# Relative-bias rows between the first weight tiles, and both parts of x in one 512-column up projection, in a hybrid decoder layer

## The chip, the core and the metric

The kernel runs on one core of one Trainium2 chip. The metric is the device time of one execution in microseconds (us). The core has five engines with instruction streams of their own: TensorE (PE in the profile; matmuls, which write to PSUM), VectorE (DVE), ScalarE (ACT), GpSimd (POOL) and SyncE (SP, which here only issues DMAs). PEld is TensorE's loading of the stationary operand. An engine works through its stream in order and waits on semaphores that other engines and DMAs raise.

## What is computed

One layer of a hybrid decoder on 256 tokens of 1024 channels, all in fp32. In the notation of the reference, cut to what matters:

```python
def reference(x, rel_bias, ...):               # x: (1, 256, 1024), rel_bias: (32, 16)
    x = x + token_mixer(rms_norm(x, norm_mix_g), ..., rel_bias)
    x = x + squared_relu_mlp(rms_norm(x, norm_mlp_g), w_up, w_down)
    return rms_norm(x, final_norm_g)

def token_mixer(xn, ...):
    proj = xn @ w_in
    (qa, ka, va, qb, kb, vb, qi, ki, wi, xc, yc, gates) = split(proj)
    y_a = moba_attention(qa, ka, va, rel_bias[:, :8])       # 8 heads of 64
    y_b = dsa_attention(qb, kb, vb, qi, ki, wi, rel_bias[:, 8:])   # index logits qi.ki choose 64 keys
    y_c = rg_lru(causal_depthwise_conv(xc), ...) * gelu(yc)
    g = sigmoid(gates)
    merged = g[0] * (y_a @ w_pa) + g[1] * (y_b @ w_pb) + g[2] * (y_c @ w_pc)
    return merged @ w_o

def squared_relu_mlp(xn, w_up, w_down):        # 1024 -> 4096 -> 1024
    return square(relu(xn @ w_up)) @ w_down
```

To the logits of both attentions the bias `rel_bias[t5_bucket(t - s)]` is added: a row of the small table, chosen by the distance of query and key.

## The kernel before

**Products in three passes.** TensorE's fast fp32 form rounds its operands. So every operand is split in two: hi is the rounded value (a ScalarE copy, line 134), lo is what is left over (a VectorE subtraction, line 135). Each product is hi x hi, hi x lo and lo x hi (`PASSES`, line 189), all added up in one PSUM tile.

**Weights** come as 512 KB half tiles `raw` over SP's queue (`load`, line 142), five of which fit; ScalarE and VectorE split them to hi and lo, six each. One weight tile (two halves) serves one PSUM tile.

**Two layouts.** `fmajor` (line 191) keeps the weights stationary and streams the 256 tokens: output channels on the partitions, 256 columns a matmul, two halves `c` of 128 output channels next to one another in a PSUM tile of 512 columns; `ks` restricts it to some of the eight blocks k of 128 input channels. `tmajor` (line 203) streams 512 weight columns with the activations stationary; down projection (line 777) and gates do the like.

**Order.** A scheduler sets every engine's order by priorities and its own estimate of times; weights are raised by `AHEAD`, evacuations of PSUM by `EVAC`. Two stretches are in manual order: the start (line 288; all engines but SP), which builds the normalised input xnh and xnl, the index queries `ps_qi` of weight tiles 0 and 1, the index keys `ps_kw` and the norm's factors (y_n on GpSimd, line 323), and TensorE's part from the output projection into the MLP (line 721).

**Relative bias** (lines 359 to 379), outside the manual stretch: `tab` (32 x 16 values and a row of NEG) and `oh` (a one-hot matrix of buckets, 33 x 384) are loaded over SP's queue; ScalarE makes `ohr` and `tabh`, VectorE `tabl`; two matmuls `psr` of 384 columns give a row of biases for every head, 8 times over; VectorE copies it (`rrow`), and a DMA on GpSimd's queue writes it many times to a scratch table `toep` in HBM, from which `load_bias` reads shifted rows for the attentions.

**Index logits** `l_i` (lines 415 to 418) take the index queries and the keys `keysh`, `keysl`, made from `ki` by `pair_keys` on ScalarE and VectorE. The **recurrent branch** has conv tiles ps_xc, second-branch tiles ps_yc, and gate matmuls `ps_ri` (line 509) that take xch and xcl.

**Into the MLP.** `residual(t, h)` (line 692) adds the output projection to x, transposes four blocks on TensorE (`tp`, line 173), and forms x2h on ScalarE (line 180) and x2l on VectorE (line 186). The first two up projections are cut in two at k: blocks 0 to 3 of tile 0, then `residual(1, 1)`, blocks 0 to 3 of tile 1, then blocks 4 to 7 of both (lines 744 to 751).

**The MLP** runs over 16 groups g of 256 hidden channels. The up projection of a group is one tile `ps_up` (48 matmuls of 256 columns, line 199). `squares` (line 759): ScalarE Relu from PSUM, ScalarE Square to hh, VectorE product, VectorE difference hl. The down projection of group g - 2 follows: 24 matmuls of 512 columns into four tiles pd. Three PSUM accumulation tiles (`acc_tile`) take turns.

## Time and profile before

| | |
|---|---|
| runs of the kernel | 455.03, 454.80, 454.54 us; median 454.8 us |
| the profiled execution | 456.36 us, of which the span of the trace is 454.6 us |
| granted TensorE clock, mean | 0.999 |
| busy: TensorE, VectorE, ScalarE, GpSimd | 445.2 (98%), 338.0 (74%), 267.0 (59%), 24.6 (5%) us |
| chain of work that ended last | TensorE 92%, DMA 2%, VectorE 2%, ScalarE 2% |
| HBM | 81.11 MB read, 1.83 MB written, 182 GB/s over the span |

Busy times are sums over an engine's instructions in the profiled execution. The chain of work that ended last is followed back from the last instruction, at each step to what released it; here it runs along TensorE nearly throughout. In a timeline a row gives the start, the length of a run of like instructions with the modelled end of the last, the engine and line, out<-in, the number of instructions (x), and in brackets how long the engine was idle before and on whom it waited. Since matmuls are pipelined, the pace of one is read from starts, not from ends.

### The profile page before, as it was taken

The numbers are of one execution on the slowest core, as the hardware profiler recorded it, in microseconds if no ns is written. First come the engines' busy times: TensorE is split into PE (matmuls) and PEld (weight loads), VectorE is DVE, ScalarE is ACT, GpSimd is POOL, SyncE is SP. The second block draws the span as 40 slices with busy tenths as digits, with TensorE's granted clock in tenths as the row PEclk, the third lists the DMA queues.
The fourth block names the chain that finished last, engine by engine and source line by source line (L and its number), as shares of the span: only waits on it lengthen the run. The fifth ranks groups of instructions, "written<-read, shape, count | busy, mean of one in ns | idle before, by whom it ended". The sixth has DMA issues, their size and how long they took to land.

```text
span 454.6 us, 7382 instructions
## 1 busy us (share of the span) xinstructions
PE 445.2 (98%) x2738; PEld 400.6 (88%) x2738; DVE 338.0 (74%) x656; ACT 267.0 (59%) x442; POOL 24.6 (5%) x61
## 2 busy tenths in 40 slices
PE   8998999999999999999999999999999999999994
PEld 8997889989988888888888889999999999999984
DVE  6798989999989999965888586655555555555545
ACT  6848398865368789665644466444444444444453
POOL 5700030000010100000000000000000000000000
PEclk9999999999999999999999999999999999999999
DMA  7877857525855453545555744555555565555202
GB/s 261 326 242 272 264 174 236 180 96 175 272 163 181 138 187 117 201 154 177 186 175 189 231 160 149 185 189 190 189 184 191 188 189 187 192 187 190 81 1 92
DMA packets 23840, 83.42 MB, mean 184 GB/s; under 512 B 2987, under 2 KB 3020, under 8 KB 23804
## 3 DMA queue, kind: packets, MB, share of 16 engines
q1 hardware_dynamic: 22700, 80.05, 53.5%
q0 software_dynamic: 960, 2.88, 2.2%
q8 instruction: 21, 0.34, 0.3%
q14 instruction: 15, 0.12, 0.1%
q10 hardware_dynamic: 144, 0.02, 0.0%
HBM read 81.11 MB, written 1.83 MB: 182 GB/s over the span
## 4 chain that ended last, share of the span: by engine, by line
PE 92%; DMA 2%; DVE 2%; ACT 2%; issue 1%; ACTq 0%; DVEq 0%
PE ps_up L199 20%; PE pd L777 19%; PE ps_g L209 14%; PE ps_p L209 7%; PE po L209 5%; PE ps_qa L199 3%; PE ps_qb L199 3%; PE ps_ka L199 3%; PE ps_kb L199 3%; PE ps_vb L209 2%; PE ps_va L209 2%; PE ps_qi L304 2%; DMA raw<-wts 2%; PE ps_yc L199 2%; PE ps_qi L199 1%; DMA sp<-small 1%
## 5 line engine op out<-in xcount | busy, mean ns | idle before, releaser
L135 DVE TENSOR_TENSOR lo<-raw,hi 128x1024 fp32r<-128x1024 f32 (+1 forms) x146 | 174.3, 1208 | 82.8 <-ACT hi L134 82.0
L134 ACT ACTIVATE hi<-raw 128x1024 fp32r<-128x1024 f32 (+1 forms) x146 | 149.7, 1045 | 124.9 <-PE pd L777 42.8
L777 PE MATMUL pd<-hi,hh 128*128 128x512 f32 (+1 forms) x128 | 49.4, 387 | 0.0
L777 PE MATMUL pd<-hi,hl 128*128 128x512 f32 (+1 forms) x128 | 49.4, 387 | 0.0
L777 PE MATMUL pd<-lo,hh 128*128 128x512 f32 (+1 forms) x128 | 49.2, 386 | 0.0
L199 PE MATMUL ps_up<-x2h,hi 128*128 128x256 f32 x256 | 36.6, 283 | 0.0
L199 PE MATMUL ps_up<-x2h,lo 128*128 128x256 f32 x256 | 36.6, 283 | 0.0
L199 PE MATMUL ps_up<-x2l,hi 128*128 128x256 f32 x256 | 36.6, 283 | 0.0
L199 PEld LDWEIGHTS ps_up<-x2h,hi 128*128 128x128 f32 x256 | 34.1, 191 | 1.0
L199 PEld LDWEIGHTS ps_up<-x2h,lo 128*128 128x128 f32 x256 | 33.3, 192 | 0.0
L199 PEld LDWEIGHTS ps_up<-x2l,hi 128*128 128x128 f32 x256 | 33.3, 192 | 0.0
L209 PE MATMUL ps_g<-hi,xnh 128*128 128x512 f32 x96 | 31.2, 395 | 0.0
L209 PE MATMUL ps_g<-hi,xnl 128*128 128x512 f32 x96 | 30.5, 393 | 0.0
L209 PE MATMUL ps_g<-lo,xnh 128*128 128x512 f32 x96 | 30.0, 391 | 0.0
L777 PEld LDWEIGHTS pd<-lo,hh 128*128 128x128 f32 x128 | 24.1, 188 | 5.0
L777 PEld LDWEIGHTS pd<-hi,hh 128*128 128x128 f32 x128 | 24.1, 188 | 4.5
L777 PEld LDWEIGHTS pd<-hi,hl 128*128 128x128 f32 x128 | 24.1, 188 | 4.4
L209 PEld LDWEIGHTS ps_g<-lo,xnh 128*128 128x128 f32 x96 | 18.0, 188 | 3.7
L209 PEld LDWEIGHTS ps_g<-hi,xnl 128*128 128x128 f32 x96 | 17.9, 188 | 3.4
L209 PEld LDWEIGHTS ps_g<-hi,xnh 128*128 128x128 f32 x96 | 17.8, 188 | 3.4
L168 POOL TENSOR_TENSOR ssq_n<-q_n 128x1 f32<-128x1 f32 x2 | 0.4, 192 | 279.8 <-ACT scr_n L166 279.8
L665 ACT ACTIVATE g<-ps_g,rh 128x512 f32<-128x512 f32 x12 | 8.2, 683 | 11.0 <-PE ps_g L209 10.9
(371 smaller groups left out, 823.7 us busy)
## 6 DMA issues: line engine op xcount, KB each, us to landing
raw<-wts SPq DMA_DIRECT2D x142, 512.0 KB, 4.8
x<-xf SPq DMA_DIRECT2D x4, 256.0 KB, 5.0
raw<-wts SPq DMA_DIRECT2D x4, 256.0 KB, 6.3
x<-x SPq DMA_DIRECT2D x2, 512.0 KB, 3.9
biasb<-toep POOLq DMA_DIRECT2D x8, 128.0 KB, 3.0
biasa<-toep POOLq DMA_DIRECT2D x8, 128.0 KB, 3.0
out<-o SPq DMA_DIRECT2D x2, 512.0 KB, 2.6
toep<-rrow POOLq DMA_DIRECT2D x1, 766.0 KB, 8.3
```

The source lines that it names most:

```text
L134: nc.scalar.activation(hi, raw, AF.Copy)
L135: nc.vector.tensor_sub(lo, raw, f(hi))
L168: nc.gpsimd.tensor_add(ssq, q[:, 0:1], q[:, 1:2])
L199: nc.tensor.matmul(pv[:, c, :], ww[a][:, k, :], xx[b][:, k, :], start=(n == 0 and k == 0 and (c == 0 or not part)), stop=(n == 2 and k == ...
L209: nc.tensor.matmul(ps, xx[b][:, k0 + k, d], ww[a][:, k, :], start=(first and n == 0 and k == 0), stop=(last and n == 2 and k == nk - 1))
L304: nc.tensor.matmul(pv[:, c, :], ww[:, k % 4, c * P:(c + 1) * P], xn[b][:, k, :], start=(i == 0 and n == 0 and k == 0 and c == 0), stop=(i ...
L665: nc.scalar.activation(g[:, t, :], ps, AF.Tanh, scale=rh[:, t:t + 1])
L777: nc.tensor.matmul(ps, hid[g][b][:, c, d], w_down[g][c][a][:, s], start=(g == (NG - LAG if o else 0) and c == 0 and m == 0), stop=(g == NG ...
```

## The change

1. **Relative bias.** The tables move into the manual start. `tab` and `oh` are loaded over ScalarE's DMA queue ahead of the first normalisation (NEG is set in row 32 alone); `bias_tables` (the split of tab into one tile `tabs`, then ohr) stands behind the last quarter of weight tile 0, ahead of the split of weight tile 1; `bias_rows` (the two psr matmuls) stands between the two halves of `ps_qi` of weight tile 1; `write_rows` (rrow, now on ScalarE, and the toep write) behind the split of kw and ahead of y_n.
2. **MLP up projection.** The two parts of the normalised x lie side by side, [block, part, token]. `wide` does one PSUM tile for 128 output channels: 8 matmuls of hi weights with 512 columns (xh | xl), so that the columns 0 to 255 hold hi x hi and the columns 256 to 511 hi x lo, and 8 of lo weights with 256 columns (xh) onto the first half. There are 32 such tiles in place of 16. `upper` adds the halves: ScalarE copies the second (u), VectorE adds it to the first (z). `squares` takes max(z, 0) x z on VectorE, then a ScalarE copy hh and a VectorE difference hl. Into the MLP three tiles are cut in two at k, with `residual(1, 1)` behind the second; its transposes take other PSUM tiles.
3. **Pad.** A filler buffer grows from 64 to 96 floats, so that every buffer behind it starts 128 bytes later.

The diff, without blank lines and without the renaming of a buffer pool (`last` to `last_`):

```diff
--- before
+++ after
@@ -107,14 +107,14 @@
         return tmp(name, 2 * n, dt).rearrange("p (j s) -> p j s", j=2)
-    nc.gpsimd.memset(fill.tile([P, 64], F32, name="filled")[:, :1], 0.0)
+    nc.gpsimd.memset(fill.tile([P, 96], F32, name="filled")[:, :1], 0.0)
     sp = tiny_.tile([P, C_END], F32, name="sp")
     nc.scalar.dma_start(sp, small)
     xt = [const.tile([P, DM], F32, name=f"x{t}") for t in range(2)]
-    ident = last.tile([P, P], F32, name="ident")
+    ident = last_.tile([P, P], F32, name="ident")
     make_identity(nc, ident)
     mhalf = tiny_.tile([P, 1], F32, name="mhalf")
     nc.gpsimd.memset(mhalf, -0.5)
@@ -200,6 +200,16 @@
                                      start=(n == 0 and k == 0 and (c == 0 or not part)),
                                      stop=(n == 2 and k == nk - 1 and (c == 1 or not part)))
+    def wide(ps, w, x2, ks=range(8)):
+        wh, wl = (z.rearrange("p (k c) -> p k c", c=P) for z in w)
+        for k in ks:
+            nc.tensor.matmul(ps, wh[:, k, :], x2[:, k], start=(k == 0), stop=False)
+        for k in ks:
+            nc.tensor.matmul(ps[:, :S], wl[:, k, :], x2[:, k, 0], start=False, stop=(k == 7))
     def tmajor(ps, w, xx, t, k0, nk, first, last):
         ww = [z.rearrange("p (k c) -> p k c", k=nk) for z in w]
@@ -211,9 +221,8 @@
-    xnh = const.tile([P, 8, S], F32R, name="xnh", tag="xnh")
-    xnl = const.tile([P, 8, S], F32R, name="xnl", tag="xnl")
-    xn = (xnh, xnl)
+    xn2 = const.tile([P, 8, 2, S], F32R, name="xn2", tag="xn2")
+    xn = xnh, xnl = xn2[:, :, 0, :], xn2[:, :, 1, :]
     xr = xt
@@ -284,6 +293,36 @@
     def split_tile(i, j):
         raw, hi, lo = loaded[i][j]
         split(hi, lo, raw)
+    tab = tiny_.tile([33, 16], F32, name="tab")
+    nc.vector.memset(tab[32:], NEG)
+    nc.scalar.dma_start(tab[:32, :], rel_bias)
+    oh = tmp("oh", 384)[:33]
+    nc.scalar.dma_start(oh, onehot)
+    psr = att_tile("psr", "t")
+    ohr = tmp("ohr", 384, F32R)[:33]
+    rrow = tmp("rrow", 384)
+    tabs = tmp("tabs", 2 * P, F32R)[:33].rearrange("p (m h c) -> p m h c", m=2, c=8)
+    def bias_tables():
+        split(tabs[:, 0], tabs[:, 1], tab[:, :, None].to_broadcast([33, 16, 8]))
+        nc.scalar.activation(ohr, oh, AF.Copy)
+    def bias_rows():
+        for m in range(2):
+            nc.tensor.matmul(psr[:, :384], tabs[:, m].rearrange("p h c -> p (h c)"), ohr, start=(m == 0), stop=(m == 1))
+    toep = dpool.tile([16, TOEP_H], F32, name="toep")
+    def write_rows():
+        nc.scalar.activation(rrow, psr[:, :384], AF.Copy)
+        n = COPIES // 8
+        nc.gpsimd.dma_start(
+            bass.AP(tensor=toep.tensor, offset=toep.offset,
+                    ap=[[n * (TOEP_W + 1), P], [TOEP_W + 1, n], [1, NB]]),
+            rrow[:, None, :NB].to_broadcast([P, n, NB]))
     with tc.manual_schedule(engines=ENGINES):
         pv = ps_q[0].rearrange("p (c t) -> p c t", c=2)
@@ -304,6 +343,7 @@
                         nc.tensor.matmul(pv[:, c, :], ww[:, k % 4, c * P:(c + 1) * P], xn[b][:, k, :],
                                          start=(i == 0 and n == 0 and k == 0 and c == 0),
                                          stop=(i == 3 and n == 2 and k == 7 and c == 1))
+        bias_tables()
         split_tile(1, 0)
         split_tile(1, 1)
@@ -313,10 +353,12 @@
                 nc.vector.tensor_add(sq[0], sq[0], sq[i])
         nc.vector.tensor_add(sqs, sq[0][:, :S], sq[0][:, S:])
         fmajor(ps_q[1], [z[1:] for z in loaded[1]], xn, cs=(0,))
+        bias_rows()
         fmajor(ps_q[1], [z[1:] for z in loaded[1]], xn, cs=(1,))
         for t in range(2):
             nc.tensor.matmul(ps_r[:, S + t:S + t + 1], sqs[:, t * P:(t + 1) * P], ones[:, :1], start=True, stop=True)
         split(kwh[:, :, :KW], kwl[:, :, :KW], kw.rearrange("p (k c) -> p k c", c=KW))
+        write_rows()
         v, y, b = (sm.tile([P, 2], F32, name=f"{n}_n1", tag=n) for n in ("v", "y", "b"))
         nc.vector.tensor_scalar(v, ps_r[:, S:S + 2], 1.0 / DM, EPS, op0=ALU.mult, op1=ALU.add)
@@ -354,29 +396,6 @@
     nc.gpsimd.memset(cmask, 0.0)
     nc.gpsimd.affine_select(out=cmask, in_=cmask, compare_op=ALU.is_ge, fill=NEG,
                             base=0, pattern=[[-1, P]], channel_multiplier=1)
-    tab = tiny_.tile([33, 16], F32, name="tab")
-    nc.vector.memset(tab, NEG)
-    nc.sync.dma_start(tab[:32, :], rel_bias)
-    oh = tmp("oh", 384)[:33]
-    nc.sync.dma_start(oh, onehot)
-    psr = att_tile("psr", "t")
-    ohr = tmp("ohr", 384, F32R)[:33]
-    nc.scalar.activation(ohr, oh, AF.Copy)
-    tabs = [tmp(f"tab{p}", P, F32R)[:33].rearrange("p (h c) -> p h c", c=8) for p in "hl"]
-    split(*tabs, tab[:, :, None].to_broadcast([33, 16, 8]))
-    for m in range(2):
-        nc.tensor.matmul(psr[:, :384], tabs[m].rearrange("p h c -> p (h c)"), ohr, start=(m == 0), stop=(m == 1))
-    rrow = tmp("rrow", 384)
-    nc.vector.tensor_copy(rrow, psr[:, :384])
-    toep = dpool.tile([16, TOEP_H], F32, name="toep")
-    n = COPIES // 8
-    nc.gpsimd.dma_start(
-        bass.AP(tensor=toep.tensor, offset=toep.offset,
-                ap=[[n * (TOEP_W + 1), P], [TOEP_W + 1, n], [1, NB]]),
-        rrow[:, None, :NB].to_broadcast([P, n, NB]))
     def load_bias(h0, name):
@@ -693,7 +712,7 @@
         s = slice(h * 512, (h + 1) * 512)
         with tc.high_priority(offset=EVAC):
             nc.vector.tensor_add(xt[t][:, s], xt[t][:, s], po[t, h])
-        ps = acc_tile(f"tp2{t}{h}") if t else att_tile(f"tp2{t}{h}", "y")
+        ps = att_tile(f"tp2{t}{h}", "lt"[h] if t else "y")
         to_features(ps, xt[t][:, s])
         with tc.high_priority(offset=EVAC):
             features_hi(ps, t, C_GMLP, x2h, h)
@@ -715,8 +734,8 @@
-    x2h = const.tile([P, 8, S], F32R, name="x2h", tag="xnh")
-    x2l = const.tile([P, 8, S], F32R, name="x2l", tag="xnl")
+    x2 = const.tile([P, 8, 2, S], F32R, name="x2", tag="xn2")
+    x2h, x2l = x2[:, :, 0, :], x2[:, :, 1, :]
     po = {(t, h): att_tile(f"po{t}{h}", "lt"[h]) for t in range(2) for h in range(2)}
     with tc.manual_schedule(engines={ET.PE}):
         w = weights()
@@ -741,14 +760,16 @@
         residual(1, 0)
         output(1, 1, 1, w)
         residual(0, 1)
-        first = []
-        for g in range(2):
-            first.append((acc_tile(f"ps_up{g}"), weights()))
-            fmajor(*first[g], (x2h, x2l), ks=range(4))
-            if g == 0:
+        w = weights() + weights()
+        first = [acc_tile(f"ps_up{c}") for c in range(3)]
+        for c in range(3):
+            wide(first[c], w[c], x2, range(4))
+            if c == 1:
                 residual(1, 1)
-        for ps, w in first:
-            fmajor(ps, w, (x2h, x2l), ks=range(4, 8))
+        for c in range(3):
+            wide(first[c], w[c], x2, range(4, 8))
+        last = w[3]
     gf = big("gf")
@@ -756,13 +777,30 @@
     pd = {(t, h): att_tile(f"pd{t}{h}", "lt"[h]) for t in range(2) for h in range(2)}
     NG, LAG = 16, 2
-    def squares(g, ps):
-        r = prob(f"r{g}", 512, F32)
-        nc.scalar.activation(r, ps, AF.Relu)
+    def upper(g):
+        z = prob(f"z{g}", 512, F32)
+        if g >= 2:
+            w = weights()
+        for c in range(2):
+            n = 2 * g + c
+            if n < 3:
+                ps = first[n]
+            else:
+                ps = acc_tile(f"ps_up{n}")
+                wide(ps, last if n == 3 else w[c], x2)
+            d = slice(c * S, (c + 1) * S)
+            u = tmp(f"u{n}", S)
+            with tc.high_priority(offset=EVAC):
+                nc.scalar.activation(u, ps[:, S:], AF.Copy)
+                nc.vector.tensor_add(z[:, d], ps[:, :S], u)
+        return z
+    def squares(g, z):
+        nc.vector.scalar_tensor_tensor(z, z, 0.0, z, op0=ALU.max, op1=ALU.mult)
         hh, hl = tmp(f"hh{g}", 512, F32R), tmp(f"hl{g}", 512, F32R)
-        nc.scalar.activation(hh, r, AF.Square)
-        nc.vector.tensor_mul(r, r, r)
-        nc.vector.tensor_sub(hl, r, f(hh))
+        nc.scalar.activation(hh, z, AF.Copy)
+        nc.vector.tensor_sub(hl, z, f(hh))
         return [z.rearrange("p (c t) -> p c t", c=2) for z in (hh, hl)]
@@ -780,12 +818,7 @@
     hid, w_down = {}, {}
     for g in range(NG):
-        if g < 2:
-            ps = first[g][0]
-        else:
-            ps = acc_tile(f"ps_up{g}")
-            fmajor(ps, weights(), (x2h, x2l))
-        hid[g] = squares(g, ps)
+        hid[g] = squares(g, upper(g))
         if g >= LAG:
             w_down[g - LAG] = weights()
             for t in range(2):
```

In the built programs the order changes as follows. Operands stand behind the arrow, x8 is the number of like instructions in a row.

ScalarE at the start, before. hi_1_128 is the split of the second half of weight tile 0, hi_0_140 and hi_1_144 are those of weight tile 1, kwh is that of kw, qi the evacuation of the first index queries:

```order
L295 ACTIVATE xnh<-x_98,sp 128x256 x2
L134 ACTIVATE hi_1_128<-raw_1_127 128x512
L134 ACTIVATE hi_0_140<-raw_0_138 128x1024
L134 ACTIVATE hi_1_144<-raw_1_142 128x1024
L311 ACTIVATE sq_179<-x_97 128x512
L311 ACTIVATE sq_180<-x_97 128x512
L311 ACTIVATE sq_181<-x_98 128x512
L311 ACTIVATE sq_182<-x_98 128x512
L134 ACTIVATE kwh<-kw 128x8x72
L278 ACTIVATE qi<-ps_qi_165 128x512
```

The same stretch of ScalarE after:

```order
L334 ACTIVATE xn_122<-x_98,sp 128x256 x2
L134 ACTIVATE hi_1_127<-raw_1_126 128x512
L134 ACTIVATE tabs<-tab 33x128
L311 ACTIVATE ohr<-oh 33x384
L134 ACTIVATE hi_0_139<-raw_0_137 128x1024
L134 ACTIVATE hi_1_143<-raw_1_141 128x1024
L351 ACTIVATE sq_178<-x_97 128x512
L351 ACTIVATE sq_179<-x_97 128x512
L351 ACTIVATE sq_180<-x_98 128x512
L351 ACTIVATE sq_181<-x_98 128x512
L134 ACTIVATE kwh<-kw 128x8x72
L320 ACTIVATE rrow<-psr 128x384
```

tabs and ohr now stand ahead of the split of weight tile 1, and rrow between kwh and qi. The DMAs of tab and oh stand ahead of ScalarE's first xn.

TensorE at the first second-branch tile ps_yc, before:

```order
L199 MATMUL ps_yc_802<-xnh,lo_0_806 128x256 x8
L199 MATMUL ps_yc_802<-xnh,hi_1_809 128x256 x8
L199 MATMUL ps_yc_802<-xnl,hi_1_809 128x256 x5
L371 MATMUL psr<-ohr,tabh 128x384
L199 MATMUL ps_yc_802<-xnl,hi_1_809 128x256 x3
L199 MATMUL ps_yc_802<-xnh,lo_1_810 128x256 x8
```

And after:

```order
L199 MATMUL ps_yc_800<-xn_122,lo_0_804 128x256 x8
L199 MATMUL ps_yc_800<-xn_122,hi_1_807 128x256 x6
L434 MATMUL l_i_418<-keysh,qi 128x256
L434 MATMUL l_i_418<-keysl,qi 128x256
L434 MATMUL l_i_418<-keysh,qil 128x256
L411 MATMUL pt_wi<-ident,wif 128x64 x2
L436 MATMUL l_i_419<-keys_157,qiq 128x256 x2
L437 MATMUL l_i_419<-keysl,qi 128x512
L199 MATMUL ps_yc_800<-xn_122,hi_1_807 128x256 x10
```

psr has left the tile, and the first index logits, which came in the tile behind it, stand in it.

TensorE at the second value tile ps_vb, before. ps_ri_746 is the second gate tile of the recurrent branch:

```order
L417 MATMUL l_i_469<-keys_158,qiq 128x256 x2
L418 MATMUL l_i_469<-keysl,qi 128x512
L509 MATMUL ps_ri_746<-xch_747,wrh 128x256
L209 MATMUL ps_vb_1003<-hi_0_954,xnh 128x512 x2
L209 MATMUL ps_vb_1003<-hi_0_954,xnl 128x512 x2
```

And after, from the last row ahead of that value tile, with the rows that follow it:

```order
L528 MATMUL ps_ri_729<-xch_730,wrl 128x256
L219 MATMUL ps_vb_1001<-hi_0_952,xn_122 128x512 x4
...
L219 MATMUL ps_vb_1001<-lo_1_969,xn_122 128x512 x2
L528 MATMUL ps_ri_744<-xch_745,wrh 128x256
L199 MATMUL ps_kb_1029<-xn_122,hi_0_1032 128x256 x8
L528 MATMUL ps_ri_744<-xcl_746,wrh 128x256
```

The second gate tile now begins behind the value tile and no longer ahead of it.

TensorE from the attention part into the MLP, before. The transposes tp are those of `residual(0, 1)` and `residual(1, 1)`, ps_up_3221 and ps_up_3272 the first two up projections:

```order
L173 MATMUL tp_3208<-ident,x_97 128x128 x4
L199 MATMUL ps_up_3221<-x2h,hi_0_3224 128x256 x4
L199 MATMUL ps_up_3221<-x2l,hi_0_3224 128x256 x4
L199 MATMUL ps_up_3221<-x2h,lo_0_3225 128x256 x4
L199 MATMUL ps_up_3221<-x2h,hi_1_3228 128x256 x4
L199 MATMUL ps_up_3221<-x2l,hi_1_3228 128x256 x4
L199 MATMUL ps_up_3221<-x2h,lo_1_3229 128x256 x4
L173 MATMUL tp_3259<-ident,x_98 128x128 x4
L199 MATMUL ps_up_3272<-x2h,hi_0_3275 128x256 x4
L199 MATMUL ps_up_3272<-x2l,hi_0_3275 128x256 x4
```

And after, where x_2913 is the tile of both parts of x:

```order
L173 MATMUL tp_3205<-ident,x_97 128x128 x4
L209 MATMUL ps_up_3242<-x_2913,hi_0_3220 128x512 x4
L211 MATMUL ps_up_3242<-x_2913,lo_0_3221 128x256 x4
L209 MATMUL ps_up_3243<-x_2913,hi_1_3224 128x512 x4
L211 MATMUL ps_up_3243<-x_2913,lo_1_3225 128x256 x4
L173 MATMUL tp_3262<-ident,x_98 128x128 x4
L209 MATMUL ps_up_3244<-x_2913,hi_0_3232 128x512 x4
L211 MATMUL ps_up_3244<-x_2913,lo_0_3233 128x256 x4
L209 MATMUL ps_up_3242<-x_2913,hi_0_3220 128x512 x4
L211 MATMUL ps_up_3242<-x_2913,lo_0_3221 128x256 x4
```

Behind the last transposes stood 24 matmuls on blocks 0 to 3 and then those on blocks 4 to 7; now 8 stand there, 4 of them wide, and the wide ones on blocks 4 to 7 follow.

## Rows read from the trace of the kernel before

**Rows 1.** The page: busy us, share of the span, number of instructions.

```profile
PE 445.2 (98%) x2738; PEld 400.6 (88%) x2738; DVE 338.0 (74%) x656; ACT 267.0 (59%) x442; POOL 24.6 (5%) x61
```

**Rows 2.** What TensorE waited for, whole span: us in total, times, longest us.

```profile
PE psr L371 <- ACT tabh L134: 1.5, 1, 1.5
```

**Rows 3.** The chain of waits in the MLP: start us, us, what.

```profile
303.12 5.75 PE ps_up L199 x48
308.87 5.47 PE pd L777 x24
```

**Rows 4.** Windows, MLP: stretch, us, busy PE, PEld, DVE, ACT, POOL, clock, DMA, GB/s.

```profile
286.00:432.00 146.00, 146.00 (x939) 133.54 (x938) 79.82 (x78) 68.62 (x79) 0.00 (x0) 1.00 0.55 179
```

**Rows 5.** Lines by form, whole span: busy us, mean ns, idle before.

```profile
L761 ACT ACTIVATE r<-ps_up 128x512 f32<-128x512 f32 x16 | 9.5, 594 | 0.0
L499 DVE SCALAR_TENSOR_TENSOR xc<-xp,sp,xc 128x256 f32<-128x256 f32 x12 | 5.2, 478 | 0.0
L297 DVE SCALAR_TENSOR_TENSOR xnl<-x,sp,xnh 128x256 fp32r<-128x256 f32 x8 | 3.5, 479 | 3.2 <-ACT xnh L295 3.2
...
L594 DVE CUSTOM_DVE_ANT_0 zb<-l_b,b2b 128x256 f32<-128x256 f32 x8 | 3.1, 420 | 0.0
```

**Rows 6.** Timeline of TensorE in the tile ps_yc: start us, us, what, idle before.

```profile
38.00 1.12 PE L199 MATMUL ps_yc<-xnh,hi 128*128 128x256 f32 x8
...
41.23 0.43 PE L371 MATMUL psr<-ohr,tabh 33*128 33x384 f32 x1 [1.52 <-ACT tabh L134]
```

**Rows 7.** Timeline of VectorE ahead of the index keys.

```profile
34.22 0.69 DVE L400 TENSOR_TENSOR xp<-ps_xc,rr 128x512 f32<-128x512 f32 x1
...
37.34 1.23 DVE L135 TENSOR_TENSOR lo<-raw,hi 128x1024 fp32r<-128x1024 f32 x1 [1.30 <-ACT hi L134]
```

**Rows 8.** Timeline of TensorE around the second gate tile ps_ri.

```profile
59.08 0.40 PE L418 MATMUL l_i<-keysl,qi 128*128 128x512 f32 x1
59.49 0.39 PE L509 MATMUL ps_ri<-xch,wrh 128*128 128x256 f32 x1
59.98 0.73 PE L209 MATMUL ps_vb<-hi,xnh 128*128 128x512 f32 x2
```

**Rows 9.** Timeline of ScalarE at the start, and its two bias instructions.

```profile
4.55 0.91 ACT L295 ACTIVATE xnh<-x,sp 128x256 fp32r<-128x256 f32 x2 [1.90 <-DMA sp<-small]
...
12.19 1.06 ACT L134 ACTIVATE hi<-raw 128x1024 fp32r<-128x1024 f32 x1 [0.50 <-DMA raw<-wts]
...
24.06 0.52 ACT L366 ACTIVATE ohr<-oh 33x384 fp32r<-33x384 f32 x1
...
40.89 0.29 ACT L134 ACTIVATE tabh<-tab 33x128 fp32r<-33x128 f32 x1
```

**Rows 10.** Timeline of TensorE at weight tile 1.

```profile
13.81 1.12 PE L199 MATMUL ps_qi<-xnh,hi 128*128 128x256 f32 x8
```

**Rows 11.** Timeline of SP's DMA issues: weight tile 0's last quarter, weight tile 1.

```profile
4.54 0.33 SPq L226 DMA_DIRECT2D raw<-wts  x1
4.92 1.32 SPq L142 DMA_DIRECT2D raw<-wts  x2
```

**Rows 12.** The chain of waits at the start.

```profile
0.72 3.80 DMA sp<-small
```

**Rows 13.** Timeline of GpSimd's queue.

```profile
49.20 0.94 POOL L376 DMA_DIRECT2D toep<-rrow  x1 [25.88 <-DVE rrow L373]
```

**Rows 14.** The page's DMA issues: KB each, median us from issue to landing.

```profile
toep<-rrow POOLq DMA_DIRECT2D x1, 766.0 KB, 8.3
```

**Rows 15.** Timelines of TensorE, ScalarE and VectorE into the MLP.

```profile
271.79 0.72 PE L199 MATMUL ps_up<-x2h,hi 128*128 128x256 f32 x4
...
272.07 1.14 ACT L180 ACTIVATE x2h<-tp,sp 128x128 fp32r<-128x128 f32 x4 [2.11 <-PE tp L173]
...
273.25 1.13 DVE L186 SCALAR_TENSOR_TENSOR x2l<-tp,sp,x2h 128x128 fp32r<-128x128 f32 x4 [1.48 <-ACT x2h L180]
```

**Rows 16.** DMA issues of the first 16 us: KB each, us to landing.

```profile
tab<-rel_bias SPq DMA_DIRECT2D x1, 2.0 KB, 7.4
```

More of the change, by code (lines that the diff above doesn't have):

```diff
@@ L70, in layer @@
     t1 = ctx.enter_context(tc.tile_pool(name="t1", bufs=4))
-    last = ctx.enter_context(tc.tile_pool(name="last", bufs=1))
+    last_ = ctx.enter_context(tc.tile_pool(name="last", bufs=1))
     wk = ctx.enter_context(tc.tile_pool(name="wk", bufs=2))
```

## The prediction, made before the changed kernel ran

> **What bounds the kernel now.** I read the page's busy shares first: TensorE works 445.2 of 454.6 us, and no other engine comes near [rows 1]. Where a matrix engine is that full, an edit can save in two ways only: fewer or shorter matmuls, or less idle time of TensorE. The list of what TensorE waited for comes next. It holds one large item in the middle of the program, 1.5 us before the relative-bias matmul psr, which waited for ScalarE's tabh [rows 2]. Third, the chain of waits through the MLP: it runs along TensorE alone, 48 up-projection matmuls of 256 columns in 5.75 us, then 24 down-projection matmuls of 512 columns in 5.47 us [rows 3]. The windows show that there TensorE is busy for 146.00 of 146.00 us at a granted clock of 1.00, its higher level of 2.4 GHz, VectorE for 79.82 and ScalarE for 68.62 [rows 4]. So VectorE and ScalarE have room in the MLP, and every nanosecond off TensorE there is off the end.
>
> **The MLP up projection.** A 256-column matmul takes 5.75/48 = 0.1198 us, a 512-column one 5.47/24 = 0.2279 us [rows 3]. The group of 48 short ones becomes 16 long and 16 short: 16 x 0.2279 + 16 x 0.1198 = 5.563 us, 0.187 less. There are 16 groups: **-2.99 us**. The 0.2279 belongs to matmuls of another place, so I bound the new one from both sides: no better than that row, no worse than two short ones (0.2396, which would save nothing). I take the row, since in both kinds a new 128x128 weight tile stands behind every matmul, and the columns stream from one contiguous row in both.
> The trace thus gives 2 x 119.8 - 227.9 = 11.7 ns for each merged pair. The Trainium skill, "TensorE: Matmul & The Clock Gate", section "Wait — 56ns, not 53.3ns?", states that a warm matmul takes its columns at 2.4 GHz plus about 2.5 ns. An estimate by that page is 256 merged pairs x 2.5 ns = 0.64 us in place of 2.99. The trace doesn't agree: 256 columns at 2.4 GHz are 106.7 ns, and its rows have 119.8. By the page the whole sum would be 2.35 us smaller.
>
> **What the MLP pays off TensorE.** Before, ScalarE evacuates 512 columns with Relu in 0.594 us [rows 5]. Now, twice a group, ScalarE copies 256 columns and VectorE adds the other 256; then VectorE squares in one instruction in place of its multiplication. For the added VectorE work the nearest row is a VectorE instruction on 256 columns, 0.420 us [rows 5]: 0.84 us a group of 5.56 + 5.47 = 11.0, on an engine that is busy 55% there. ScalarE's bound is two evacuations of 0.594 in place of one. An accumulation tile is wanted again after half a group, a down projection and another half, 2.8 + 5.5 + 2.8 = 11.1 us; copy, add, square, copy and subtract, each below 0.7, are behind it in 3 to 4. Cost **0**; the cover is some 7 us.
>
> **The psr wait goes.** psr now stands between the two halves of the second index-query tile, and its tables are made right behind the first weight tile's splits. TensorE's 1.52 us before psr [rows 6] vanish: **-1.5 us**. Its two matmuls (0.43 us each by the model of their ends, 0.37 from start to start [rows 6]) only move. What is late next at the old place? There the index logits l_i now interrupt the tile yc after six matmuls of a run: 38.00 + 6 x 0.12 [rows 6] + 0.75 for the earlier psr, so at 39.5. Their keys keysl come on VectorE right behind xp (34.22, 0.69) and one weight split (1.23) [rows 7] where three splits stood between: 34.22 + 0.75 + 0.69 + 1.23 + four short ones of 0.2 to 0.4, some 38.0. Slack 1.5.
> The new order also takes the second gate matmul ps_ri, before squeezed in between l_i and the value tile ps_vb, to a later place. Around it TensorE stands idle twice: between 59.08 + 0.23 and 59.49, 0.18 us, and between 59.49 + 0.12 and 59.98, 0.37 us [rows 8]. I expect both to go: **-0.5 us** (bounds 0 and -0.55).
>
> **The start.** ScalarE now makes tabh (0.29) and ohr (0.52) ahead of the split of the second weight tile, which starts at 12.19 after 0.50 us of waiting for its DMA [rows 9]; 0.81 - 0.50 = 0.31 us later. That split ends at 13.25, and TensorE reaches its first use at 13.81 [rows 10]: slack 0.56, so it holds. The DMAs are the risk. In the built program hardware transfers take turns on eight semaphores, and an issue on a taken one waits until the earlier transfer has landed: SP's eighth, at 4.54 [rows 11], waited for sp, which landed at 0.72 + 3.80 = 4.52 [rows 12]. tab and oh now take two turns, so SP's sixth issue waits for sp already, and the second weight tile's first half, issued at 4.92 before [rows 11], waits for tab. ScalarE issues tab in its idle time from 2.65 to 4.55 [rows 9]; by sp's 3.80 us it lands between 6.45 and 8.35, so that issue slips by 1.5 to 3.4 us. It need not land later: it took 12.19 - 4.92 = 7.27 us, against 3.80 for sp, so some 3.5 us of it went by in the queue behind other transfers. **0 us**, bounds 0 and 2.9 (3.4 less the slack of 0.56, if nothing is absorbed). The kw tile waits for oh in the same way and is wanted later.
> rrow moves from VectorE to ScalarE, a copy of some 0.5 us behind the split of kw and ahead of qi, where no matmul is short of ScalarE. The toep write (0.94 us of POOL's queue [rows 13]) now stands ahead of y_n there; it goes out as soon as rrow is made, while y_n still waits for TensorE's sums of squares and VectorE's v_n: **0**, bound 0.9. The 766 KB of toep need 8.3 us [rows 14] and fall near 20 to 29 instead of 49 to 58, where weights are also on their way; I take 0, and up to 2 with the unseen.
>
> **The handover to the MLP.** This edit costs. After the last residual's transposes TensorE has only the k 0 to 3 part of the third tile: 4 x 0.2279 + 4 x 0.1198 = 1.39 us, from 271.79 to 273.18. Then the 512-column matmuls want the high and the low part of k 4 to 7 at once. Before, the first pass took only the high parts (ScalarE, 272.07 to 273.21); the low ones came from VectorE at 273.25 to 274.38 [rows 15] while TensorE was still on high ones. Now the fourth matmul can't start before 274.38, where it would have at 273.18 + 3 x 0.2279 = 273.86: **+0.5 us** (bounds 0, if VectorE follows ScalarE instruction by instruction, and 1.2).
>
> **The pad.** It shifts every later buffer by 128 bytes. A VectorE instruction of one form takes 478 ns with operands at an odd offset (xc) and 479 with aligned ones (xnl) [rows 5]; **0**.
>
> **Sum.** -2.99 - 1.5 - 0.5 + 0.5 = -4.49 us. The profiled execution, 456.36 us with its span of 454.6, would take 451.9; the median of the runs is 1.56 lower, so 454.8 becomes **450.3 us**.
>
> **Rivals.**
> 1. *Merging saves little*: the streaming is the cost, not the number of matmuls. With nothing saved the sum is -1.5: 453.3. For it: no 512-column matmul of this place is in the trace. Against it: 24 long ones take 5.47, not 5.75 [rows 3]. It spans 452.6 to 453.3. The page's 0.64 us would make it 452.65. Chance 0.10.
> 2. *The wait at psr only moves*, to the start or to the logits. If the second weight tile lands late, or l_i waits for its keys as psr did for tabh, the gain of 1.5 is spent: 451.8; with the start's bound of 2.9, 453.2. For it: slacks of 0.56 and 1.5 are thin. Chance 0.16.
> 3. *SP stands behind tab* (slower). tab's own transfer took 7.4 us before [rows 16]. Issued between 2.65 and 4.55 it would land at 10.05 to 11.95; if the second weight tile still needs its 7.27 us after that, it lands at 17.3 to 19.2 instead of 12.19, and TensorE waits 4.6 to 6.5: 454.9 to 456.8. It decides the sign once that issue falls later than 4.92 + 0.56 + 4.49 = 9.97. Against it: tab stood in SP's own queue behind seven weight transfers; now it is on ScalarE's, where sp took 3.80, and by 10 us the queue is emptier. Chance 0.06.
> 4. *The holes at 59 us stay and the handover costs its bound*: 0.5 + 0.7 more, 451.5. Inside the forecast's range.
>
> **How the numbers follow.** The forecast, 449.4 to 451.6 with the slacks holding, has 0.65, rival 4 among it; rival 1 has 0.10, rival 2 0.16, rival 3 0.06, and 0.03 is left for a wait that I don't see. The low end has the handover at 0 and half a microsecond more from TensorE's small holes: 449.3. The high end takes in rival 2 up to 452.9 and part of rival 1. A measurement of this kernel can tell some 0.2% (0.9 us) from no change. Faster is below 453.9, which holds all but rival 3 and the rest: 0.91; same 0.03; slower 0.06.
>
> **What would show it.** Right: no psr in the list of TensorE's waits; chain pieces of 5.56 us for 32 up-projection matmuls; one wait of about 0.5 us for x2l at the handover; the second weight tile's split starting before 13. Wrong: a 512-column up matmul above 0.235 us (rival 1); a TensorE wait for hi near 14 or for keysl near 39 (rival 2); SP's issue of the second weight tile later than 10 (rival 3); a TensorE wait for the MLP's evacuation in every group.

## The result

| | median | lowest to highest | runs |
|---|---|---|---|
| before | 454.91 us | 454.54 to 455.63 | 4 |
| changed | 450.37 us | 449.99 to 450.61 | 4 |

The ratio is 0.9897, 95% interval 0.988 to 0.9915: 4.5 us or 1.0% faster. The forecast was 450.3 us. The sum came out; as the experiments show, two of its terms were wrong by nearly the same amount in opposite directions, so that hitting it this closely is partly luck. Two executions of 735.58 us (the changed kernel, in a later group) and 1557.16 us (the pad) are left out of the medians.

The page of the changed kernel, as [rows 1]: 256 matmuls fewer, 5.2 us less work for TensorE, 11.6 us more for VectorE.

```profile
PE 440.0 (98%) x2482; PEld 384.8 (86%) x2482; DVE 349.6 (78%) x687; ACT 267.7 (60%) x459; POOL 24.1 (5%) x61
```

What TensorE waited for, over the whole span, as [rows 2]. psr is gone from the list; a wait for x at the handover into the MLP is new.

```profile
PE ps_qi L343 <- ACT hi L134: 1.4, 1, 1.4
PE warm L131 <- DVE zero L129: 1.1, 1, 1.1
PE ps_up L209 <- DVE x L186: 0.2, 1, 0.2
```

The chain of waits through one group of the MLP, as [rows 3]. L209 are the wide matmuls, L211 those of lo weights. The 32 of a group take 1.81 + 0.95 + 1.84 + 0.95 = 5.55 us (5.56 from start to start), where 48 took 5.75.

```profile
288.68 1.81 PE ps_up L209 x8
290.49 0.95 PE ps_up L211 x8
291.44 1.84 PE ps_up L209 x8
293.28 0.95 PE ps_up L211 x8
294.24 5.47 PE pd L815 x24
```

The windows over the MLP, as [rows 4]: TensorE is still busy throughout at the higher level. VectorE's share has gone from 55% to 62%, ScalarE's from 47% to 48%.

```profile
283.21:426.60 143.39, 143.39 (x730) 122.50 (x729) 89.28 (x104) 69.06 (x92) 0.00 (x0) 1.00 0.56 180
```

Lines by form, as [rows 5]: the evacuation of 256 columns (add on VectorE, copy on ScalarE) and the square.

```profile
L796 DVE TENSOR_TENSOR z<-ps_up,u 128x256 f32<-128x256 f32 x32 | 13.4, 418 | 0.0
L795 ACT ACTIVATE u<-ps_up 128x256 f32<-128x256 f32 x32 | 11.8, 368 | 0.0
L800 DVE SCALAR_TENSOR_TENSOR z<-z 128x512 f32<-128x512 f32 x16 | 11.1, 691 | 0.5
```

The timelines of TensorE, ScalarE and VectorE at the handover, as [rows 15]. The wide matmuls of blocks 4 to 7 start at 270.22, where the ones ahead are through at 269.37 + 4 x 0.12 = 269.85; and the first four of them last until 271.39, 1.17 us, where four take 0.92. Hole and stretching make 0.37 + 0.25 = 0.62 us.

```profile
268.00 0.60 PE L173 MATMUL tp<-ident,x 128*128 128x128 f32 x4
...
269.37 0.63 PE L211 MATMUL ps_up<-x,lo 128*128 128x256 f32 x4
270.22 1.34 PE L209 MATMUL ps_up<-x,hi 128*128 128x512 f32 x4 [0.22 <-DVE x L186]
271.39 0.64 PE L211 MATMUL ps_up<-x,lo 128*128 128x256 f32 x4
...
268.63 1.14 ACT L180 ACTIVATE x<-tp,sp 128x128 fp32r<-128x128 f32 x4 [2.05 <-PE tp L173]
...
269.81 1.13 DVE L186 SCALAR_TENSOR_TENSOR x<-tp,sp,x 128x128 fp32r<-128x128 f32 x4 [1.40 <-ACT x L180]
```

The start, as [rows 9 to 11]: SP issues the second weight tile at 5.89 in place of 4.92, behind issues at 4.57, 4.94 and 5.41, and ScalarE still splits it at 11.96, before 12.19.

```profile
4.57 0.33 SPq L235 DMA_DIRECT2D raw<-wts  x1
...
5.89 0.91 SPq L142 DMA_DIRECT2D raw<-wts  x2
...
11.16 0.29 ACT L134 ACTIVATE tabs<-tab 33x128 fp32r<-33x128 f32 x1
11.96 2.27 ACT L134 ACTIVATE hi<-raw 128x1024 fp32r<-128x1024 f32 x2
...
13.08 2.18 PE L199 MATMUL ps_qi<-xn,hi 128*128 128x256 f32 x16
```

TensorE at the index logits, as [rows 6]: they come at 38.54 without a wait.

```profile
37.82 0.88 PE L199 MATMUL ps_yc<-xn,hi 128*128 128x256 f32 x6
38.54 0.28 PE L434 MATMUL l_i<-keysh,qi 128*128 128x256 f32 x1
```

The two profiled executions took 456.36 and 450.61 us, 5.75 apart, and the medians only 4.5. That difference was the first thing to be cleared up.

### The profile page after: what moved, and what is told of

It reads as the page before. It is cut to its first block, busy times and chain, and to the rows that moved or that the text cites. A ratio compares the mean times of both kernels' runs of the same rounds, so it can differ in the third digit from the quotient of the medians.

```text
span 448.8 us, 6931 instructions
## 1 busy us (share of the span) xinstructions
PE 440.0 (98%) x2482; PEld 384.8 (86%) x2482; DVE 349.6 (78%) x687; ACT 267.7 (60%) x459; POOL 24.1 (5%) x61
## 4 chain that ended last, share of the span: by engine, by line
PE 88%; DMA 4%; POOL 3%; DVE 2%; ACT 1%; issue 1%; SPq 0%; ACTq 0%; DVEq 0%; POOLq 0%
PE pd L815 19%; PE ps_g L219 15%; PE ps_up L209 13%; PE ps_p L219 7%; PE ps_up L211 7%; PE po L219 5%; DMA raw<-wts 3%; PE ps_qa L199 3%; PE ps_qb L199 3%; PE ps_kb L199 3%; PE ps_ka L199 3%; PE ps_va L219 2%; PE ps_vb L219 2%; DVE lo L135 1%; DMA x<-xf 1%
## 5 line engine op out<-in xcount | busy, mean ns | idle before, releaser
L209 PE MATMUL ps_up<-x,hi 128*128 128x512 f32 x256 | 64.7, 393 | 0.2 <-DVE x L186 0.2
L209 PEld LDWEIGHTS ps_up<-x,hi 128*128 128x128 f32 x256 | 46.7, 188 | 9.3 <-DVE x L186 0.4
L219 PE MATMUL ps_g<-hi,xn 128*128 128x512 f32 x192 | 53.7, 392 | 0.0
L219 PEld LDWEIGHTS ps_g<-hi,xn 128*128 128x128 f32 x192 | 35.6, 188 | 6.8
L211 PEld LDWEIGHTS ps_up<-x,lo 128*128 128x128 f32 x256 | 35.3, 190 | 2.7
L211 PE MATMUL ps_up<-x,lo 128*128 128x256 f32 x256 | 36.2, 282 | 0.0
L219 PE MATMUL ps_g<-lo,xn 128*128 128x512 f32 x96 | 30.2, 392 | 0.0
L219 PEld LDWEIGHTS ps_g<-lo,xn 128*128 128x128 f32 x96 | 17.9, 188 | 3.6
L796 DVE TENSOR_TENSOR z<-ps_up,u 128x256 f32<-128x256 f32 x32 | 13.4, 418 | 0.0
L795 ACT ACTIVATE u<-ps_up 128x256 f32<-128x256 f32 x32 | 11.8, 368 | 0.0
```

The lines of the kernel that those rows point to most:

```text
L209: nc.tensor.matmul(ps, wh[:, k, :], x2[:, k], start=(k == 0), stop=False)
L211: nc.tensor.matmul(ps[:, :S], wl[:, k, :], x2[:, k, 0], start=False, stop=(k == 7))
L219: nc.tensor.matmul(ps, xx[b][:, k0 + k, d], ww[a][:, k, :], start=(first and n == 0 and k == 0), stop=(last and n == 2 and k == nk - 1))
L795: nc.scalar.activation(u, ps[:, S:], AF.Copy)
L796: nc.vector.tensor_add(z[:, d], ps[:, :S], u)
```

## The experiments

The theory that was tested: the gain is the sum of two edits that don't touch one another, of which the MLP brings 2.5 to 2.8 (2.99 less the handover) and the bias 2.0 (the wait at psr and two holes). The rivals were those of the prediction. All times are medians; the kernel before ran beside each group and had 454.9, 455.3 and 454.9 us.

**The bias edit alone.**

```diff
+    nc.scalar.dma_start(tab[:32, :], rel_bias)
...
+        bias_tables()
         split_tile(1, 0)
...
         fmajor(ps_q[1], [z[1:] for z in loaded[1]], xn, cs=(0,))
+        bias_rows()
         fmajor(ps_q[1], [z[1:] for z in loaded[1]], xn, cs=(1,))
...
+        write_rows()
...
-    nc.sync.dma_start(tab[:32, :], rel_bias)
```

> The kernel before with the relative-bias edit alone. Theory: TensorE's 1.52 us wait before psr and, where the scheduler sets the same order as in the changed kernel, the two holes near 59.5 and 60 us (0.55 together) go, so 2.0 us less than before in the median, and no wait for hi or keysl takes their place. Rival (the wait only moves): at most 0.5 us less, with a new wait of TensorE of about 1.5 us at the second weight tile or the index logits. Rival (SP stands behind tab): slower than before, with the second weight tile issued later than 10 us.

Measured: 452.89 us (452.28 to 453.65), ratio 0.9949, interval 0.9931 to 0.9968: 2.0 less, as the theory has it. No wait for keys or hi took psr's place, and both rivals are out. But its trace doesn't bear out the terms; this follows below.

**The MLP edit alone.**

```diff
+    x2 = const.tile([P, 8, 2, S], F32R, name="x2", tag="xn2")
...
+        for c in range(3):
+            wide(first[c], w[c], x2, range(4, 8))
...
-            fmajor(ps, weights(), (x2h, x2l))
-        hid[g] = squares(g, ps)
+        hid[g] = squares(g, upper(g))
```

> The kernel before with the MLP edit alone (both parts of x in one 512-column matmul, and the evacuation and squares that go with it). Theory: a group's up projection takes 5.56 us in place of 5.75, 16 x 0.187 = 2.99 us less, and the handover into the MLP costs 0.2 to 0.5: 2.5 to 2.8 us less in the median. Rival (the streaming is the cost, not the number of matmuls): at most 0.6 us less, with wide matmuls at 0.235 us or more. Rival (the evacuation turns into a wait): TensorE waits for an accumulation tile in every group, and the gain is gone.

Measured: 452.08 us (451.84 to 453.11), ratio 0.9935, interval 0.9909 to 0.996: 2.8 less. The wide matmuls run at 1.81/8 = 0.226 to 1.84/8 = 0.230 us, near the 0.228 of 512-column matmuls elsewhere [rows 3]; the rival that merging saves little is out, and TensorE waits for no accumulation tile. The two edits add up: 2.0 + 2.8 = 4.8, against 4.5 for both.

**The pad alone.**

```diff
-    nc.gpsimd.memset(fill.tile([P, 64], F32, name="filled")[:, :1], 0.0)
+    nc.gpsimd.memset(fill.tile([P, 96], F32, name="filled")[:, :1], 0.0)
```

> The kernel before with the pad alone: every later buffer 128 bytes further on. Theory: nothing, within 0.3 us of the kernel before, and the same mean durations by line. Rival (an alignment counts): a difference of more than 0.5 us, with changed means of VectorE's or ScalarE's instructions on 1024 columns.

Measured: 454.67 us, ratio 0.9989, interval 0.9973 to 1.0005: nothing. By form, the splits of 1024 columns have the same means as before (ScalarE 1056 ns for 1057, VectorE 1221 for 1222).

**The kernel before, traced again.** Nothing is changed in it.

> The kernel before once more, unchanged, for a second trace of it. In its first trace TensorE's matmuls ran at 0.215 us for 256 columns until 10.3 us; in the trace of the changed kernel they ran at 0.12 from 6.3 us on, and the first matmul of the second weight tile came at 13.08 in place of 13.81. Theory: where the lower clock ends is a matter of the single execution, so that this trace can have it elsewhere than at 10.3, and the execution's own time moves with it by up to 1 us. Rival: it belongs to the kernel (the start of before is slower by about 0.9 us in every execution); then this trace has 10.3 and 13.8 again.

> The kernel before once more, for another trace of the hole at psr and of the start. Theory: its execution time is 440.9 us plus the start of TensorE on the second weight tile plus the hole before psr, as in the first traces (456.36 = 440.87 + 13.81 + 1.68; 453.70 = 440.97 + 12.73 + 0), to 0.2 us. Rival: other holes differ as much, and the sum misses by more than 0.5 us.

Measured: 454.63 and 454.53 us; the traced executions took 453.70 and 454.90. The first theory holds: in the second trace TensorE takes its 256-column matmuls at 0.12 us from 6.16 on, and in the third at 0.21 us until about 10.2 again, with its start on the second weight tile at 13.98. That the slow pace is the lower clock isn't shown: the granted clock is 1.00 there too (last section). What matters more is that both traces have no wait at psr. The list of what TensorE waited for, in the trace of 453.70 us:

```profile
PE ps_qi L304 <- ACT hi L134: 1.3, 2, 0.9
PE warm L131 <- DVE zero L129: 1.1, 1, 1.1
```

ScalarE's timeline there shows why. tabh stands behind splits that wait for raw weights. Here two of them wait 0.88 and 0.58 us and tabh is made at 37.74:

```profile
31.46 1.06 ACT L134 ACTIVATE hi<-raw 128x1024 fp32r<-128x1024 f32 x1 [0.88 <-DMA raw<-wts]
33.10 1.06 ACT L134 ACTIVATE hi<-raw 128x1024 fp32r<-128x1024 f32 x1 [0.58 <-DMA raw<-wts]
...
37.74 0.29 ACT L134 ACTIVATE tabh<-tab 33x128 fp32r<-33x128 f32 x1
```

In the first trace the same two waited longer, and tabh came at 40.89 [rows 9]:

```profile
33.50 1.06 ACT L134 ACTIVATE hi<-raw 128x1024 fp32r<-128x1024 f32 x1 [1.89 <-DMA raw<-wts]
36.25 1.06 ACT L134 ACTIVATE hi<-raw 128x1024 fp32r<-128x1024 f32 x1 [1.68 <-DMA raw<-wts]
```

So the hole before psr depends on when raw weights land. In five traces with psr at its old place and tabh on ScalarE it was 1.67, 1.10, 0.21, 0 and 0 us, 0.6 in the mean, which five such values fix poorly; 0 stands for psr coming 0.09 late without a wait. With it and the start of TensorE on the second weight tile the traced executions can be laid out (us; the rest is what is left of the time; the last two kernels come below and cost nothing against the changed one):

| trace | time | start on weight tile 1 | hole before psr | rest |
|---|---|---|---|---|
| before, the first | 456.36 | 13.81 | 1.67 | 440.88 |
| before, again | 453.70 | 12.73 | 0 | 440.97 |
| before, a third time | 454.90 | 13.98 | 0 | 440.92 |
| the pad alone | 454.57 | 13.56 | 0.21 | 440.80 |
| the bias edit alone | 452.53 | 12.76 | - | 439.77 |
| the MLP edit alone | 453.11 | 13.48 | 1.10 | 438.53 |
| changed, the first | 450.61 | 13.08 | - | 437.53 |
| changed, again | 450.93 | 13.89 | - | 437.04 |
| changed, tab and oh on GpSimd's queue | 450.61 | 13.41 | - | 437.20 |
| changed, toep behind y_n | 450.50 | 13.38 | - | 437.12 |

Four traces of the old program agree to 0.2 us in the rest, as expected. By the rest, the MLP edit brings 2.4 us, and the bias edit 1.1 in its own trace. That trace has a new hole, 0.17 us before the first gate matmul ps_ri and 0.10 behind it; the first trace of the changed kernel has it too (0.29 and 0.10), the other three of the changed kernel in the table don't, and set beside the MLP edit alone they give the bias edit 438.53 - 437.12 = 1.4. So 1.1 to 1.4 us belong to the program; what the bias edit brings beyond that is the hole before psr, 0.6 in the mean and 1.67 in the one trace that the prediction read. The 5.75 us between the first traces are 0.73 of start, 1.67 of hole and 3.35 of rest. The start varies by more than a microsecond in either program; its means are 13.6 in the six traces with the old start of the bias (13.81, 12.73, 13.98, 13.56, 13.48 and, from the kernel with tabh on GpSimd, 13.88) and 13.5 in the six with the new one (13.08, 13.89, 12.76 and, from the kernels below, 14.37, 13.41, 13.38).

**The changed kernel, traced again.**

> The changed kernel once more, unchanged, beside the three that follow and for a second trace of its start. Expected: a median near 450.4 us, no wait of TensorE for psr, one hole of 0.38 us at the handover into the MLP, 5.56 us for a group's up projection. Where TensorE takes up the second weight tile is open: 13.08 us in its first trace, 12.73, 13.48, 13.56 and 13.81 in four traces whose start is that of the kernel before.

> The changed kernel once more, for another trace. Theory: its execution time is 437.2 to 437.6 us plus the start of TensorE on the second weight tile, as in 450.61 = 437.53 + 13.08, with no hole at psr; the start itself lies between 12.7 and 14.4. Rival: a hole elsewhere, of more than 0.4 us, differs between its executions.

Measured: 450.30 and 450.87 us. Only the second left a trace that can be read. It has the start at 13.89 and the handover's hole of 0.37; its rest of 437.04 lies 0.16 below the span that was expected and 0.49 below the first trace, of which 0.39 is the hole around the first gate matmul ps_ri (0.29 before it, at 48.63, and 0.10 behind it), missing here. So a hole of the rival's kind does differ between executions, by just under the 0.4 it was set at.

**tabh off ScalarE's queue, in the kernel before.**

```diff
-    split(*tabs, tab[:, :, None].to_broadcast([33, 16, 8]))
+    tb = tab[:, :, None].to_broadcast([33, 16, 8])
+    nc.gpsimd.tensor_copy(tabs[0], tb)
+    nc.vector.tensor_sub(tabs[1], tb, f(tabs[0]))
```

> The kernel before with tabh made by GpSimd, which is idle at that time, in place of ScalarE; psr and the rest of the bias stay where they were. This takes away what makes psr wait, without moving work to the start. In four traces with the old place of psr TensorE's hole before it was 1.68, 1.10, 0.21 and 0 us. Theory: the wait depends on when raw weights land ahead of tabh in ScalarE's queue, and differs between executions; with tabh off that queue the first psr waits for nothing, and the median falls by about the mean of the four holes, 0.75 us (between 0.3 and 1.2, less what the second psr may wait for tabl). Rival (the first trace is typical): 1.5 us less. The two holes near the second gate tile, 0.55 us together, should stay, since nothing there is changed on purpose.

Measured: 453.28 us (452.66 to 453.56), ratio 0.996, interval 0.9945 to 0.9974: 1.6 less, more than the theory had, and near the number of the rival. Neither psr waits; the first still stands in the tile ps_yc, the second among the index logits. The trace shows that the number doesn't come from the wait alone: the scheduler reorders what follows, and the two holes [rows 8] are gone with it. TensorE's timeline at that place:

```profile
55.60 0.40 PE L420 MATMUL l_i<-keysl,qi 128*128 128x512 f32 x1
55.83 0.28 PE L511 MATMUL ps_ri<-xch,wrh 128*128 128x256 f32 x1
55.95 0.62 PE L209 MATMUL ps_vb<-hi,xnl 128*128 128x512 f32 x2
```

The expectation that the holes stay was wrong. Its rest is 453.54 - 13.88 = 439.66, 1.3 below that of before, without a psr wait on either side. The rows have 0.66 of it in the two holes and the 0.11 behind them, and some 0.45 in the second psr, which starts at 42.44, 0.01 us behind a 64-column matmul at 42.43, and sets back what follows by only 0.1 us, where one in the tile costs 0.56 (see below). So the two holes, the largest part of the bias edit's steady gain, go with a new order around the recurrent branch, and that can be had without moving the rows to the start. As the edit changes both the engine and the order, it doesn't isolate the wait, as it was meant to.

**The matmuls of lo weights first at the handover**, in the changed kernel.

```diff
         for c in range(3):
-            wide(first[c], w[c], x2, range(4, 8))
+            wide(first[c], w[c], x2, range(4, 8), lo_first=(c == 0))
...
+        if lo_first:
+            for k in ks:
+                nc.tensor.matmul(ps[:, :S], wl[:, k, :], x2[:, k, 0], start=False, stop=False)
         for k in ks:
-            nc.tensor.matmul(ps, wh[:, k, :], x2[:, k], start=(k == 0), stop=False)
+            nc.tensor.matmul(ps, wh[:, k, :], x2[:, k], start=(k == 0), stop=(lo_first and k == 7))
```

> The changed kernel, with one order changed at the handover: of the first tile's blocks 4 to 7 the four matmuls that need only the high part of x come ahead of the four wide ones. Theory: the 0.38 us hole of TensorE comes from x's low part on VectorE, which is late by less than the 4 x 0.12 = 0.48 us that now stand ahead, so the hole goes: 0.3 to 0.4 us less than the changed kernel. Rival: the hole belongs to the high part or to the wide matmul itself; then it stays, and so does the time.

Measured: 450.02 us (449.6 to 450.95) beside 450.30 (450.11 to 450.84) for the changed kernel in the same group: 0.3 less, as the theory has it, though the two ranges overlap. The trace is clearer than the median. TensorE's timeline has no hole, and the eight wide matmuls behind run on:

```profile
268.89 0.60 PE L173 MATMUL tp<-ident,x 128*128 128x128 f32 x4
269.25 1.17 PE L212 MATMUL ps_up<-x,hi 128*128 128x512 f32 x4
270.26 0.64 PE L215 MATMUL ps_up<-x,lo 128*128 128x256 f32 x4
270.74 0.64 PE L210 MATMUL ps_up<-x,lo 128*128 128x256 f32 x4
271.21 2.10 PE L212 MATMUL ps_up<-x,hi 128*128 128x512 f32 x8
```

From the last transposes into the MLP to the start of the last matmul it is 174.25 us (268.89 to 443.14), against 174.77 in the changed kernel (268.00 to 442.77): 0.52 of the 0.62 come back. The four matmuls that need only the high part start at 270.74, as soon as the ones ahead are through (270.26 + 4 x 0.12), so the low part of x was what the wide matmuls waited for. This kernel has the lowest median of all that ran, by a step smaller than the spread of its runs.

**tab and oh on GpSimd's queue**, in the changed kernel.

```diff
-    nc.scalar.dma_start(tab[:32, :], rel_bias)
+    nc.gpsimd.dma_start(tab[:32, :], rel_bias)
-    nc.scalar.dma_start(oh, onehot)
+    nc.gpsimd.dma_start(oh, onehot)
```

> The changed kernel with the loads of tab and oh on GpSimd's queue, so that they take no turns on the hardware semaphores: SP issues the second weight tile's first half at 4.9 in place of 5.89. Theory: that slip of 1 us was absorbed by the queue of transfers, so the second weight tile is split no earlier than by 0.2 us and the time stays within 0.3 us. Rival: the slip counts; then TensorE takes up the second weight tile 0.5 to 1 us earlier and the kernel is that much faster.

Measured: 450.62 us (450.54 to 451.54) beside 450.30: 0.3 more, at the edge of what was expected and within the spread of the runs; the rival's gain isn't there. SP issues the second weight tile 1.04 us earlier, and its split starts no earlier than 11.96. The split waits for no DMA there; by the profile the first half took 7.3 us from issue to landing and 6.1 in the changed kernel, so it landed near 12.2 and 12.0, and the slip was absorbed on the way:

```profile
4.85 1.38 SPq L142 DMA_DIRECT2D raw<-wts  x2
...
12.25 1.04 ACT L134 ACTIVATE hi<-raw 128x1024 fp32r<-128x1024 f32 x1
```

**toep behind y_n**, in the changed kernel.

```diff
-        write_rows()
         nc.gpsimd.tensor_tensor(y, v, mhalf.to_broadcast([P, 2]), op=ALU.pow)
+        write_rows()
```

> The changed kernel with the write of toep behind y_n in GpSimd's queue instead of ahead of it. In the trace of the changed kernel y_n came at 21.35, 1.0 us later than before, right behind the toep issue. Theory: y_n moves back by 0.9 us, TensorE waits for nothing there, and the time is the same within 0.3 us. Rival: the norm's factors and the index keys behind y_n are on the path; then up to 0.9 us less.

Measured: 450.50 us (449.99 to 450.88) beside 450.30: 0.2 more, no change beyond the spread. GpSimd's timeline, first of the changed kernel, then of this one: in the first y_n comes right behind the toep issue, in the second it comes 0.6 us earlier, although TensorE's start was 0.3 us later there; nothing is late for y_n.

```profile
20.42 0.93 POOL L322 DMA_DIRECT2D toep<-rrow  x1
21.35 0.86 POOL L365 TENSOR_TENSOR y_n<-v_n,mhalf 128x2 f32<-128x2 f32 x1
```

```profile
20.75 0.73 POOL L364 TENSOR_TENSOR y_n<-v_n,mhalf 128x2 f32<-128x2 f32 x1 [0.33 <-DVE v_n L363]
21.44 0.92 POOL L322 DMA_DIRECT2D toep<-rrow  x1
```

## Why the prediction was right, point by point

**The MLP: right in mechanism and size.** Forecast -2.99 for the matmuls and +0.5 for the handover, so -2.5. The MLP edit alone brings -2.8 in the median and -2.4 by the rests; a group takes 5.55 us for the forecast 5.563. Without the handover's cost the matmuls bring 2.4 + 0.6 = 3.0. The estimate of 0.64 us by the Trainium skill ("TensorE: Matmul & The Clock Gate", section "Wait — 56ns, not 53.3ns?", some 2.5 ns above the columns) isn't borne out here: the trace has 0.95/8 = 118.8 ns for 256 columns, 12 ns above 106.7, and 226 to 230 ns for 512, 13 to 17 ns above 213.3.

**The evacuation: right.** 0.418 us for VectorE's added instruction (forecast 0.420), VectorE busy 62% of the MLP, no wait of TensorE.

**The handover: right.** Forecast +0.5, found 0.37 of hole and 0.25 of stretching, 0.52 of it recovered by another order. VectorE's low parts started behind ScalarE's fourth high part, as in [rows 15].

**The psr wait: the step that failed.** The term -1.5 was read from one execution and taken for the program's. The hole was 1.67 there, 0 to 1.10 in four other traces and 0.6 in the mean. The prediction had the hint before it: this execution lay 1.56 us above the median of its runs, and I subtracted that excess and the whole wait from the median all the same, though most of the excess was the wait.

**The holes at the gate matmul: right that they go, too small as a term.** Forecast -0.5. The steady part of the bias edit is -1.1 to -1.4. By the rows it is the two holes and 0.11 behind them (0.66), 0.2 at the first matmul of ps_yc, 0.4 because two psr in a row cost less than two apart, and 0.2 between the first matmuls of ps_g and ps_m (115.24 us in the third trace of before, 115.03 with the bias edit), which isn't explained; the hole before the first ps_ri takes 0.27 back where it stands. In the third trace of before each psr comes 0.09 late and takes 0.37 us to the next start, and the row behind that comes 0.1 late, 1.12 for both:

```profile
39.12 0.76 PE L199 MATMUL ps_yc<-xnl,hi 128*128 128x256 f32 x5
39.81 0.43 PE L371 MATMUL psr<-ohr,tabh 33*128 33x384 f32 x1
40.18 0.62 PE L199 MATMUL ps_yc<-xnl,hi 128*128 128x256 f32 x3
40.64 1.12 PE L199 MATMUL ps_yc<-xnh,lo 128*128 128x256 f32 x8
...
44.80 0.40 PE L199 MATMUL ps_yc<-xnh,lo 128*128 128x256 f32 x2
45.14 0.44 PE L371 MATMUL psr<-ohr,tabl 33*128 33x384 f32 x1
45.51 0.62 PE L199 MATMUL ps_yc<-xnh,lo 128*128 128x256 f32 x3
45.96 0.28 PE L415 MATMUL l_i<-keysh,qi 128*128 128x256 f32 x1
```

In the changed kernel both take 16.69 - 16.14 = 0.55, with 0.08 ahead and 0.09 behind, 0.72:

```profile
16.14 0.62 PE L315 MATMUL psr<-ohr,tabs 33*128 33x384 f32 x2
16.69 0.50 PE L199 MATMUL ps_qi<-xn,hi 128*128 128x256 f32 x2
```

So the bias came to -0.6 for the wait and -1.1 to -1.4 for the rest, -1.7 to -2.0 for the forecast -2.0: an overestimate of 0.9 and an underestimate of 0.6 to 0.9. Which part of the steady gain comes from where psr stands, and which from the scheduler's order, stays open: with tabh on GpSimd it was 1.3, and the first psr was still in the tile.

**The start: right at 0, by another road.** The prediction had ScalarE issue tab between 2.65 and 4.55 and SP's issue of the second weight tile wait for it. tab was issued at 1.24 and took 3.6 us (sp 3.8), so it had landed at 4.84 and SP never waited for it; rival 3's 7.4 didn't come into play. The slip of 0.97 us, below the forecast 1.5 to 3.4, is that SP's sixth issue waits for sp, as the prediction had it, and two more issues stand behind it. It was absorbed, as the run without it shows. The terms add up to -4.1 to -4.4 (-1.1 to -1.4, -2.4, -0.6), for -4.5 measured, interval -5.5 to -3.9.

**toep, y_n and the pad: right at 0**, though y_n did come later by the queue.

## What to carry to other kernels

Set a profiled execution beside the median before a wait is read from it: here most of the excess of one execution was that very wait, and what ends it (here DMAs of weights ahead in an in-order queue) tells whether it belongs to the program. On an engine that is full, count the issues: merging two short matmuls that share weights brought 11 to 12 ns a pair, 0.6% of the time with the handover paid, as long as both halves of the wide operand are ready; where one is late, put the work that needs only the other in between. And where a scheduler sets the order, a moved block changes the order elsewhere, and as much of the gain can lie there as in the block.
